# Two MLP stages: weights of the plain groups moved ahead of the operand sums, modulation steps spread, a last part of four tiles

## Chip, core and metric

One core of a Trainium2 chip (trn2) runs the whole program. The metric is the device time of one launch in microseconds, lower is better. Times of the kernel before are those of three runs, and one more execution was taken with the hardware profiler.

## The reference, cut to what matters

Two layers run over 640 positions: 128 context tokens and 512 latent tokens, which share the weights but have modulation vectors of their own. Everything is float32. The change touches only the second half of each layer, the gated MLP:

```python
xn2 = rmsnorm(x, norm2) * (1 + scale2) + shift2          # 640 x 1024
u   = dwconv3(xn2 @ w_up, ffn_conv_w)                    # w_up: 1024 x 5632, width-3 conv over positions
a, bval = u[..., :D_FF], u[..., D_FF:]                   # D_FF = 2816
x   = x + gate2 * ((silu(a) * bval) @ w_down)            # w_down: 2816 x 1024
```

and, inside layer 0's MLP, a part of the modulation vector of layer 1, `silu(c) @ w_ada[1] + b_ada[1]`, of which six blocks of 128 rows (blocks 10 to 15) are computed there. What stands ahead of the MLP (adaLN norm, recurrence, short convolution, attention, merge, output projection) is the same in both kernels.

## The kernel before, in words

**Layout.** Activations are kept transposed, channels on the 128 partitions and positions along the free axis; a matmul has 320 positions (half of them) as moving columns. To keep float32 accuracy every operand and every weight is split into a high part (a cast to fp32r on ScalarE) and a low part (a subtraction on VectorE); a product is three matmuls, high*high, high*low, low*high. The helper `split` (lines 115 and 116) does both halves, for weights into the tiles `whi` and `wlo` (six buffers each), for operands into `Xh`/`Xl` and `Fh`/`Fl`, for the activated MLP tiles into `fh`/`fl`. Weights land in four raw buffers `wraw` (two more, `T`, in the MLP), all issued from SyncE's queue in order.

**Queues.** The source is written as one sequence with generators that are advanced by hand (`next`, `run`). The framework plans at build time in which order each engine gets its instructions: an earlier place in the source is a higher priority, but an instruction whose inputs or buffer are not ready in the plan is passed by a later one. On the chip each engine then follows its planned order and waits for semaphores.

**The MLP stage** has 22 tiles of 128 hidden channels, each a pair of column groups of `w_up` (a and b).
- *Operand forms.* The two position halves of the normed input are B11, B21 (first half, computed at the end of the output projection) and B12, B22 (second half, `second`). Pairs from number 2 on use a seven-product scheme (`pair_steps`) that needs sums of the forms: T3, t2, T4, t1, each of two tiles and each split; they too are made in `second`. Six buffers `Fh`/`Fl` hold B12, T3, t2 and T4; T4 takes the buffers that B12 leaves.
- *Plain groups.* Pairs 0 and 1 (`PLAIN = 2`), four groups n = 0 to 3, are plain products over B11, B21, B12, B22 (lines 1211 to 1222): group n loads its weights at its first half and calls `finish` after its second. `finish(j, s)` is the width-3 convolution of one group (`ffn_conv`: one ScalarE, two VectorE instructions) and, with the second group of a pair, `ffn_act` (silu, product, split), which appends a tile to `Ys`.
- *Pairs.* `pair_steps` loads four raw tiles, adds them in place on VectorE (line 500) and splits seven weights a pair; it stops at three places, so that a pair's first product can be put ahead of the pair before it.
- *Down products.* `FFPARTS` cuts the 22 tiles into parts. When a part is complete its contributions to all eight output blocks (`down_steps`) run in the next part's pairs, are scaled on ScalarE (line 1232, tile `g`) and added to `x` in memory by a DMA from GpSimd. The last part is different: its eight blocks run at the end, for the first half of the positions in the order 0 to 7 and for the second half in the order 7, 6, 0 to 5, straight into `x` (line 1265), mixed with the norm of the next layer or the output. Its weights for blocks 0 to 4 are loaded and split twice, once for each half.
- *Modulation steps.* `ada_rows` makes 12 steps in layer 0's MLP, each a raw tile `in_w_rows` and two VectorE instructions that multiply and sum (line 318), and a short thirteenth. Two are taken after each pair (line 1248). Half way the vector tile `rows` is loaded again.

**PSUM.** The MLP has two banks for `Y`, one each for `Z` and `X`, two `f`, and the two `lin` that serve all stages.

Of the kernel before, what the change touches and what calls it, by code (L numbers as in the profile page):

```python
# [16 lines left out]
P = 128  # L17
# [29 lines left out]
AHEAD = (1, 4)  # L47
ADA1 = 10
ADAM = 3
FFPARTS = ((0, 3), (3, 7), (7, 11), (11, 15), (15, 19), (19, 22))  # L50

G_HG, G_CONV, G_CQ, G_CKV, G_KR, G_GATE, G_OUT, G_UP = 0, 20, 32, 35, 37, 38, 62, 70
NG = 70 + 2 * NFF
# [3 lines left out]
def hybrid_flow_kernel(ctx: ExitStack, tc: tile.TileContext, a: dict):  # L57
# [20 lines left out]
    def run(steps, n=None):  # L78
        while n is None or n > 0:
            try:  # L80
                next(steps)
            except StopIteration:
                return
            if n is not None:
                n -= 1
# [44 lines left out]
    def weights(srcs, keep=None):  # L130

        W = []
        for src in srcs:
            n = src.shape[-1] // P
            wh, wl = load_w(src, n * P, keep)
            W += [(wh[:, i * P:(i + 1) * P], wl[:, i * P:(i + 1) * P]) for i in range(n)]
        return W
# [269 lines left out]
    class Forms:  # L407
# [33 lines left out]
        def second(self, pool):  # L441
            bc = self.sq.rstd(1)
            raw = self.raw
            for q in range(2):
                for n, name in enumerate(("B12", "B22")):
                    f = raw[name, q] = form_tile(pool, F32, "fh", "xn", FHB)
                    for e in range(2):
                        norm_raw(self.l, self.which, self.sq, 1, f, e, KH * n + 2 * q + e, bc)
                    self.put(name, q, f)
            for q in range(2):  # L450
                f = raw["T3", q] = form_tile(pool, F32, "fl", "xs", FHB)
                V.tensor_tensor(f, raw["B22", q], raw["B12", q], ALU.subtract)
                self.put("T3", q, f)
            for q in range(2):
                f = raw["t2", q] = form_tile(pool, F32, "fl", "xs", FHB)
                V.scalar_tensor_tensor(f, raw["T3", q], -1.0, raw["B11", q], ALU.mult, ALU.subtract)
                self.put("t2", q, f)
            for q in range(2):
                f = raw["t2", q]
                V.scalar_tensor_tensor(f, f, -1.0, raw["B21", q], ALU.mult, ALU.subtract)  # L460
                self.put("T4", q, f)
            for q in range(2):
                f = raw["B12", q]
                V.tensor_tensor(f, raw["B11", q], f, ALU.subtract)
                self.put("t1", q, f)
            raw.clear()
# [69 lines left out]
    KEEP = KD - 3  # L536
# [453 lines left out]
    with pool_of("ap") as ap:  # L990
        rows, W, R = ada_load(ap)
# [68 lines left out]
    for l in range(DEPTH):  # L1060
# [4 lines left out]
        with pool_of("yp") as yp:  # L1065
            yB = [yp.tile([P, T + 1], F32, tag="yB", name="yB", bufs=4) for _ in range(4)]
            yC = [yp.tile([P, T], F32, tag="yC", name="yC", bufs=4) for _ in range(4)]
            with pool_of("cp") as cp, pool_of("kp") as kp:
# [10 lines left out]
                W = [mla_weights(l, 0)]  # L1079
# [15 lines left out]
            with pool_of("zp") as zp:  # L1095
# [11 lines left out]
                steps = iter(())  # L1107
# [15 lines left out]
                with pool_of("hp") as hp:  # L1123
                    if l == 0:
                        steps = chain(ada_rows(0, 16, 48, zp, lambda: ps.one("ad")),
                                      ada_rows(1, 0, ADA1, zp, lambda: ps.one("ad")))
                    else:
                        steps = ada_rows(1, 16, 48, zp, lambda: ps.one("ad"))
# [30 lines left out]
        xf = xf_.__enter__()  # L1159
        F = Forms(l, 1, sq, xf)  # L1160

        def kept(m):

            if not 0 < m <= KEEP:
                return None
            pool, tags, n = (xf, "F", 6) if m <= 3 else (wo, "k", 4)
            return lambda: [pool.tile([P, T], R32, tag=tags + t, name="keep", bufs=n) for t in "hl"]

        with pool_of("wo") as wo:
            W = {}  # L1170
# [16 lines left out]
        with pool_of("fp") as fp:  # L1187
            F.second(fp)
            sq = Squares(sq.pool)
            steps = iter(())  # L1190
            if l == 0:
                steps = ada_rows(1, ADA1, 16, fp, lambda: fp.tile([P, TP], F32, tag="u", name="pr", bufs=4)[:, 0:512])
            fconv = fp.tile([P, 3, 2 * NFF], F32, name="fconv")
            nc.sync.dma_start(fconv, a["fconv"][:, l])
            os_ = [fp.tile([P, TP + 2], F32, name=f"o{i}") for i in range(4)]
            zs = fp.tile([P, TP + 2], F32, name="z")
            for t in os_ + [zs]:
                for c0, c1 in ((0, 1), (TC + 1, TC + 3), (TP + 1, TP + 2)):
                    G.memset(t[:, c0:c1], 0.0)
            Ys, us = [], {}  # L1200

            def finish(j, s):
                us[s] = ffn_conv(s * NFF + j, os_[2 * (j % 2) + s], fp, fconv)
                if len(us) == 2:
                    Ys.append(ffn_act(us[0], us[1], fp))
                    us.clear()


            B = [F.operand("B11", "B21"), F.operand("B12", "B22")]
            held = {}  # L1210
            for n, j, tag in ((0, 0, "lin"), (1, 0, "lin"), (2, 0, "Y"), (0, 1, "Y"), (1, 1, "X"), (2, 1, "Z"),
                              (3, 0, "f"), (3, 1, "f")):
                if j == 0:
                    held[n] = weights(w_main(l, G_UP + n))
                o = (ps.bank() if tag == "lin" else ps.one(tag))[:, 0:HALF]
                for k, ((wh, wl), (xh, xl)) in enumerate(zip(held[n], B[j], strict=True)):
                    PE.matmul(o, wh, xh, start=(k == 0), stop=False)
                    PE.matmul(o, wh, xl, start=False, stop=False)
                    PE.matmul(o, wl, xh, start=False, stop=(k == KD - 1))
                put_half(os_[n], o, j)  # L1220
                if j == 1:
                    finish(n // 2, n % 2)

            def down_steps(k0, k1):
                for m in range(KD):
                    W = weights([a["w_down"][l, m][:, k * P:min(k + 4, k1) * P] for k in range(k0, k1, 4)])
                    g = fp.tile([P, T], F32, tag="u", name="g", bufs=4)
                    for j in range(2):
                        o = ps.any()
                        down_product(o[:, 0:FHALF[j].stop - FHALF[j].start], W, Ys[k0:k1], j)  # L1230
                        for c, s0, s1, s in FSEGS[j]:
                            S.mul(g[:, s0:s1], o[:, c:c + s1 - s0], modT[l][:, 40 + m, s:s + 1])  # L1232
                    G.dma_start(x[m], g, accum_op=ALU.add)  # L1233
                    yield

            ups = [pair_steps(l, G_UP + 2 * j, F, fp, os_[2 * (j % 2)], os_[2 * (j % 2) + 1], zs,
                              lambda s, j=j: finish(j, s)) for j in range(NFF)]
            next(ups[PLAIN])
            down = iter(())
            for pi, (k0, k1) in enumerate(FFPARTS):  # L1240
                last = pi == len(FFPARTS) - 1
                ahead = max(k0, PLAIN)
                for j in range(ahead, k1):
                    next(ups[j])
                    if j + 1 < NFF:
                        next(ups[j + 1])
                    run(ups[j])
                    run(steps, 2)
                    run(down, -(-KD // max(1, k1 - ahead - 1)))
                run(down)  # L1250
                if not last:
                    down = down_steps(k0, k1)
                if l == 0 and last:
                    run(steps)
                    ada_scale(1, 0)
            k0, k1 = FFPARTS[-1]
            W = {}
            for j in range(2):
                for m in both_ways(j):
                    if j == 0 or 0 <= m <= KEEP - 1:  # L1260
                        W[m] = weights([a["w_down"][l, m][:, k * P:min(k + 4, k1) * P] for k in range(k0, k1, 4)])
                    o = ps.any()
                    down_product(o[:, 0:FHALF[j].stop - FHALF[j].start], W[m], Ys[k0:k1], j)
                    for c, s0, s1, s in FSEGS[j]:
                        V.scalar_tensor_tensor(x[m][:, s0:s1], o[:, c:c + s1 - s0],
                                               modT[l][:, 40 + m, s:s + 1], x[m][:, s0:s1], ALU.mult, ALU.add)
                    sq.add(m, j)
                    if j == 1:
                        run(first, 1)
                if j == 0:  # L1270
                    if l + 1 < DEPTH:
                        X = new_X()
                        first = norm_steps(l + 1, 0, sq, 0, X)
                    else:
                        first = out_steps(sq, 0)
            run(first)
            if l + 1 < DEPTH:
                ps.phase("mla")
                run(norm_steps(l + 1, 0, sq, 1, X))
            else:  # L1280
                run(out_steps(sq, 1))
# [125 lines left out]
```

## Time and profile before

| what | value |
|---|---|
| median of three runs (lowest, highest) | 2590.28 us (2584.23, 2593.17) |
| the profiled execution, its own time | 2585.24 us |
| its span, first to last instruction | 2583.5 us |
| TensorE busy, share of the span | 2491.8 us, 96% |
| VectorE busy | 1853.4 us, 72% |
| ScalarE busy | 1333.6 us, 52% |
| MLP of layer 0, about | 846 to 1328 us of the span |
| MLP of layer 1 with the output, about | 2115 to 2583 us |

Times in the trace count from the span's start. A busy share says little on its own here: TensorE's matmuls overlap, and a stage's limit is read from the waits inside it. Line numbers (L116) are those of the listing above; PE is TensorE, DVE VectorE, ACT ScalarE, SP SyncE's queue.

### The profile page before, as it was taken

To read this page: it belongs to the slowest core of one execution; us is meant where nothing else is said; L and a number is where in the kernel's file an instruction comes from. 1 tells how busy PE (TensorE), PEld (TensorE's weight loads), DVE (VectorE), ACT (ScalarE), POOL (GpSimd) and SP (SyncE) were. 2 spreads that over 40 slices of the span, in tenths; PEclk is the share of its full clock that TensorE was granted. 3 is DMA by queue.
4 is the path that set the end of the run, shared out by engine and by line. 5 is a ranking of instruction groups with operands and counts; after the bars stand their busy time and mean duration, and the time that the engine had idled before them with its cause. 6 is when DMAs were issued, how large, how long until landed. Compare 5 with 4: busy or idle time off the path is not lost.

```text
span 2583.5 us, 44707 instructions
## 1 busy us (share of the span) xinstructions
PE 2491.8 (96%) x16942; PEld 2429.8 (94%) x16942; DVE 1853.4 (72%) x3711; ACT 1333.6 (52%) x2846; POOL 186.7 (7%) x207
## 2 busy tenths in 40 slices
PE   7999999999999899999989999999999999999997
PEld 3999999999999889999989999999999999999996
DVE  5677787787755778777677778777784468877775
ACT  3476733333324556666654766333433346766663
POOL 1000000000110000000120000000011110001011
PEclk8999999999999999999989999999999999999998
DMA  6211243333353154545432113433332323455443
GB/s 233 74 46 46 66 133 110 105 113 109 112 156 99 47 134 124 130 104 126 113 121 67 38 46 93 119 112 119 104 104 79 110 66 87 113 120 114 117 112 90
DMA packets 147498, 265.41 MB, mean 103 GB/s; under 512 B 17425, under 2 KB 32465, under 8 KB 147153
## 3 DMA queue, kind: packets, MB, share of 16 engines
q1 hardware_dynamic: 131154, 225.85, 29.5%
q0 software_dynamic: 11520, 26.22, 5.6%
q10 hardware_dynamic: 4608, 10.49, 1.3%
q8 instruction: 133, 2.18, 0.4%
q14 instruction: 83, 0.68, 0.1%
HBM read 229.68 MB, written 6.59 MB: 91 GB/s over the span
## 4 chain that ended last, share of the span: by engine, by line
PE 81%; DVE 11%; DMA 2%; ACT 2%; issue 2%; POOL 0%; DVEq 0%; SPq 0%; ACTq 0%; POOLq 0%
PE lin L148 13%; PE lin L150 13%; PE lin L149 13%; PE Y L472 3%; PE Y L474 3%; PE Y L473 3%; PE sc L625 2%; PE sc L890 2%; PE lin L978 2%; PE f L980 2%; PE lin L979 2%; PE lin L980 2%; PE f L979 2%; PE f L978 2%; DVE wlo L116 2%
## 5 line engine op out<-in xcount | busy, mean ns | idle before, releaser
L148 PE MATMUL lin<-Xh,whi 128*128 128x320 f32 x1920 | 605.1, 315 | 6.4 <-DVE th L728 5.1
L149 PE MATMUL lin<-Xl,whi 128*128 128x320 f32 x1920 | 595.4, 310 | 0.5 <-POOL Xl L379 0.5
L150 PE MATMUL lin<-Xh,wlo 128*128 128x320 f32 x1920 | 595.1, 310 | 0.0
L115 ACT CAST whi<-wraw 128x512 fp32r<-128x512 f32 (+1 forms) x578 | 349.0, 606 | 445.3 <-PE lin L149 270.7
L116 DVE TENSOR_TENSOR wlo<-wraw,whi 128x512 fp32r<-128x512 f32 (+1 forms) x578 | 389.0, 677 | 183.8 <-ACT whi L115 178.4
L148 PEld LDWEIGHTS lin<-Xh,whi 128*128 128x128 f32 x1920 | 361.3, 188 | 8.8 <-DVE th L728 6.9
L149 PEld LDWEIGHTS lin<-Xl,whi 128*128 128x128 f32 x1920 | 361.2, 188 | 0.8 <-POOL Xl L379 0.8
L150 PEld LDWEIGHTS lin<-Xh,wlo 128*128 128x128 f32 x1920 | 360.8, 188 | 0.0
L318 DVE SCALAR_TENSOR_TENSOR ad<-wraw,rows 128x512 f32<-128x512 f32 x296 | 211.6, 715 | 92.2 <-DMA wraw<-in_w_rows 88.7
L116 DVE TENSOR_TENSOR wlo<-T,whi 128x512 fp32r<-128x512 f32 x160 | 109.7, 688 | 71.5 <-ACT whi L115 70.6
L472 PE MATMUL Y<-Xh,whi 128*128 128x320 f32 x480 | 148.6, 310 | 2.5 <-ACT o L481 2.5
L474 PE MATMUL Y<-Xh,wlo 128*128 128x320 f32 x480 | 148.3, 309 | 0.0
L473 PE MATMUL Y<-Xl,whi 128*128 128x320 f32 x480 | 148.1, 309 | 0.0
L115 ACT CAST whi<-T 128x512 fp32r<-128x512 f32 x160 | 99.0, 621 | 82.5 <-DVE T L500 21.4
L1233 POOL DMA_DIRECT2D x<-g x80 | 69.2, 864 | 772.9 <-ACT g L1232 765.3
L148 PE MATMUL lin<-yh,whi 128*128 128x320 f32 x384 | 120.5, 314 | 0.7 <-ACT th L722 0.7
L978 PE MATMUL lin<-fh,whi 128*128 128x322 f32 (+1 forms) x352 | 111.0, 315 | 9.3 <-ACT fh L115 7.0
L150 PE MATMUL lin<-yh,wlo 128*128 128x320 f32 x384 | 118.8, 309 | 0.0
L149 PE MATMUL lin<-yl,whi 128*128 128x320 f32 x384 | 118.6, 309 | 0.0
L980 PE MATMUL lin<-fh,wlo 128*128 128x322 f32 (+1 forms) x352 | 110.9, 315 | 0.0
L979 PE MATMUL lin<-fl,whi 128*128 128x322 f32 (+1 forms) x352 | 110.8, 315 | 0.0
L980 PE MATMUL f<-fh,wlo 128*128 128x320 f32 (+1 forms) x352 | 110.3, 313 | 0.0
(377 smaller groups left out, 6335.6 us busy)
## 6 DMA issues: line engine op xcount, KB each, us to landing
wraw<-in_w_main SPq DMA_DIRECT2D x416, 256.0 KB, 2.7
wraw<-in_w_rows SPq DMA_DIRECT2D x160, 256.0 KB, 2.8
x<-g POOLq DMA_DIRECT2D x80, 320.0 KB, 4.7
wraw<-in_w_down SPq DMA_DIRECT2D x64, 256.0 KB, 2.8
wraw<-in_w_o SPq DMA_DIRECT2D x48, 256.0 KB, 2.7
T<-in_w_main SPq DMA_DIRECT2D x40, 256.0 KB, 2.9
wraw<-in_w_down SPq DMA_DIRECT2D x42, 192.0 KB, 2.4
ada<-in_w_ada SPq DMA_DIRECT2D x24, 256.0 KB, 6.0
```

Source lines behind the costliest of these rows:

```text
L115: S.copy(hi, x)
L116: V.tensor_tensor(lo, x, hi.bitcast(F32), ALU.subtract)
L148: PE.matmul(o, wh, xh[:, half(j)], start=(k == 0), stop=False)
L149: PE.matmul(o, wh, xl[:, half(j)], start=False, stop=False)
L150: PE.matmul(o, wl, xh[:, half(j)], start=False, stop=(k == n - 1))
L318: V.scalar_tensor_tensor(spare(), raw, 1.0, rows[:, s], ALU.mult, ALU.mult, accum_out=part[:, j, m - m0, s:s + 1])
L472: PE.matmul(o, wh[:, c], xh, start=start and k == 0, stop=False, skip_group_check=True)
L473: PE.matmul(o, wh[:, c], xl, start=False, stop=False, skip_group_check=True)
L474: PE.matmul(o, wl[:, c], xh, start=False, stop=stop and k == KH - 1, skip_group_check=True)
L978: PE.matmul(o, wh, fh[:, FHALF[j]], start=(k == 0), stop=False)
L979: PE.matmul(o, wh, fl[:, FHALF[j]], start=False, stop=False)
L980: PE.matmul(o, wl, fh[:, FHALF[j]], start=False, stop=(k == n - 1))
```

## The change

1. `Forms.second` ends after the four forms B12 and B22; the sums and their splits become a method `sums`, called after the loop over the plain groups. So the plain groups' loads and splits stand ahead of the sums in the source.
2. The plain loop no longer calls `finish`. Pair 0's two convolutions come after `sums`, pair 1's after pair 2's first product.
3. In layer 0 the modulation steps are taken one after each pair from pair 3 on, in place of two after each pair from pair 2 on.
4. The last two parts of `FFPARTS` are (15, 18) and (18, 22) in place of (15, 19) and (19, 22).
5. In the last part each block's weights are one load of four tiles, made once; blocks 1 to 5 are held in the six `Fh`/`Fl` buffers of the forms (`kept` with its new argument), and the second half loads nothing.

```diff
-FFPARTS = ((0, 3), (3, 7), (7, 11), (11, 15), (15, 19), (19, 22))
+FFPARTS = ((0, 3), (3, 7), (7, 11), (11, 15), (15, 18), (18, 22))
...
                     self.put(name, q, f)
+
+        def sums(self, pool):
+            raw = self.raw
             for q in range(2):
                 f = raw["T3", q] = form_tile(pool, F32, "fl", "xs", FHB)
...
-        def kept(m):
+        def kept(m, n0=3):
...
-            pool, tags, n = (xf, "F", 6) if m <= 3 else (wo, "k", 4)
+            pool, tags, n = (xf, "F", 6) if m <= n0 else (wo, "k", 4)
...
                 put_half(os_[n], o, j)
-                if j == 1:
-                    finish(n // 2, n % 2)
+            F.sums(fp)
...
+            for n in range(2):
+                finish(0, n)
             next(ups[PLAIN])
+            for n in range(2):
+                finish(1, n)
...
                     run(ups[j])
-                    run(steps, 2)
+                    if j >= FFPARTS[1][0]:
+                        run(steps, 1)
                     run(down, -(-KD // max(1, k1 - ahead - 1)))
...
-                    if j == 0 or 0 <= m <= KEEP - 1:
-                        W[m] = weights([a["w_down"][l, m][:, k * P:min(k + 4, k1) * P] for k in range(k0, k1, 4)])
+                    if j == 0:
+                        W[m] = weights([a["w_down"][l, m][:, k0 * P:k1 * P]], kept(m, KEEP))
```

## Rows read from the trace of the kernel before

**Rows 1.** The page, part 1: engine, busy us (share of span), instructions.
```profile
PE 2491.8 (96%) x16942; PEld 2429.8 (94%) x16942; DVE 1853.4 (72%) x3711; ACT 1333.6 (52%) x2846; POOL 186.7 (7%) x207
```

**Rows 2.** Busy time by stretch: stretch, length, engines busy (instructions), clock, DMA.
```profile
870.00:883.00 13.00, 8.24 (x40) 7.98 (x39) 11.33 (x17) 6.66 (x11) 0.00 (x0) 0.74 0.11 41
902.00:913.00 11.00, 7.28 (x30) 6.79 (x29) 9.13 (x18) 5.34 (x10) 0.00 (x0) 0.69 0.43 130
913.00:1003.00 90.00, 80.81 (x527) 78.48 (x526) 69.54 (x126) 53.31 (x122) 7.04 (x8) 0.98 0.50 131
1003.00:1289.00 286.00, 286.00 (x1943) 285.84 (x1942) 207.95 (x326) 184.45 (x409) 27.75 (x35) 1.00 0.51 119
1289.00:1299.00 10.00, 6.52 (x32) 5.99 (x31) 6.38 (x14) 4.92 (x11) 0.90 (x2) 0.83 0.08 21
2139.00:2150.00 11.00, 6.25 (x33) 5.99 (x33) 10.75 (x16) 5.97 (x9) 0.00 (x0) 0.84 0.14 48
2150.00:2537.00 387.00, 387.00 (x2630) 386.84 (x2629) 287.63 (x443) 256.58 (x568) 34.53 (x40) 1.00 0.48 116
2537.00:2548.00 11.00, 7.52 (x34) 7.26 (x33) 6.56 (x15) 4.86 (x10) 1.53 (x2) 0.69 0.06 18
```

**Rows 3.** Timeline, TensorE: start, us, instruction, [idle before <-releaser].
```profile
876.25 0.64 PE L1219 MATMUL f<-Xh,wlo 128*128 128x320 f32 x1 [4.76 <-DVE wlo L116]
...
886.72 0.31 PE L472 MATMUL Z<-Fh,whi 128*128 128x320 f32 x1
...
958.52 0.41 PE L472 MATMUL Y<-Xh,whi 128*128 128x320 f32 x1 [2.52 <-ACT o L481]
958.77 0.30 PE L473 MATMUL Y<-Xl,whi 128*128 128x320 f32 x1
958.91 0.31 PE L474 MATMUL Y<-Xh,wlo 128*128 128x320 f32 x1
...
2154.41 0.31 PE L472 MATMUL Z<-Fh,whi 128*128 128x320 f32 x1
```

**Rows 4.** Timeline, ScalarE and VectorE, layer 0, plain groups.
```profile
862.45 0.62 ACT L115 CAST whi<-wraw 128x512 fp32r<-128x512 f32 x1 [0.24 <-PE Y L1218]
...
866.04 0.61 ACT L115 CAST whi<-wraw 128x512 fp32r<-128x512 f32 x1
...
875.51 1.29 DVE L116 TENSOR_TENSOR wlo<-wraw,whi 128x512 fp32r<-128x512 f32 x2
```

**Rows 5.** The chain that ended last: start, us, what; first norm of either layer.
```profile
853.07 2.84 DVE xn L403 x6
...
2121.88 2.84 DVE xn L403 x6
```

**Rows 6.** VectorE by line and shape, 846 to 912 us: count, busy us, mean ns.
```profile
L116 DVE TENSOR_TENSOR wlo<-wraw,whi 128x512 fp32r<-128x512 f32 x8 | 5.4, 687 | 0.3 <-ACT whi L115 0.2
L959 DVE SCALAR_TENSOR_TENSOR u<-o,fconv,u 128x642 f32<-128x642 f32 x6 | 5.2, 884 | 0.9 <-ACT u L958 0.9
...
L116 DVE TENSOR_TENSOR Xl<-xn,Xh 128x640 fp32r<-128x640 f32 x4 | 3.3, 819 | 0.0
L318 DVE SCALAR_TENSOR_TENSOR pr<-wraw,rows 128x512 f32<-128x512 f32 x4 | 2.7, 685 | 0.0
```

**Rows 7.** Timeline, SyncE's queue, 936 to 990 us.
```profile
945.84 0.38 SPq L313 DMA_DIRECT2D rows<-c_keep  x1
...
970.01 5.02 SPq L316 DMA_DIRECT2D wraw<-in_w_rows  x2
```

**Rows 8.** Timeline, TensorE, first wait of layer 0's last part.
```profile
1293.60 0.41 PE L978 MATMUL lin<-fh,whi 128*128 128x322 f32 x1 [3.48 <-ACT fh L115]
```

**Rows 9.** Timeline, end of layer 1: VectorE and TensorE.
```profile
2556.31 0.56 DVE L116 TENSOR_TENSOR wlo<-wraw,whi 128x384 fp32r<-128x384 f32 x1
...
2561.29 0.94 PE L249 MATMUL lin<-dg,ones 128*128 128x128 f32 x6 [1.70 <-DVE dg L243]
```

## The prediction, made before the changed kernel ran

> **What bounds the kernel now.** I read the page first. TensorE is busy for 96% of the span, VectorE for 72% [rows 1]: the time is TensorE's list of matmuls plus the places where it stands still, and the change adds and removes no matmul. So the next view is the busy time by stretch [rows 2]. In the long undisturbed stretches (1003 to 1289 in layer 0, 2150 to 2537 in layer 1) TensorE never idles, the granted clock is 1.00, and 1943 matmuls in 286.0 us give 0.147 us a matmul. A stretch that holds n matmuls and is longer than 0.147 n has lost the rest, idle time and half-speed matmuls together. By this rule the MLPs lose
>
> - 870 to 883: 13.0 - 40 x 0.147 = 7.1 us, and 2139 to 2150 in layer 1: 6.1;
> - 902 to 913, layer 0 only: 6.6;
> - 913 to 1003, layer 0 only: 90.0 - 527 x 0.147 = 12.4;
> - 1289 to 1299: 5.3, and 2537 to 2548: 6.0.
>
> Together 43.5 us, all in places that the change touches. The timeline says what TensorE waited for [rows 3, 8]: the low half of group 3's weights, which VectorE had not made (4.76 us); in the last part the last activated tile (3.48 us). The half speed is seen in the clock of these stretches, 0.62 to 0.84 [rows 2]: after waits of 3.5 us and more matmuls run at the 1.2 GHz level for a while, while after the 2.52 us wait at 958 the second step is back at 0.14 us [rows 3].
>
> **A. Plain groups.** Group 3's first cast ended at 863.07 and its second at 866.65, but VectorE subtracted only at 875.51 [rows 4]: the sums, their splits and pair 0's convolution stood in between. With the weights ahead in the source this wait goes. But it does not follow that 7.1 and 6.1 us are won, since VectorE has worked without a break from its first norm at 853.07 (2121.88 in layer 1) [rows 5] and is next in line. What it must do before pair 2's first product over T3 can start: 8 norms at 2.84/6 = 0.47, 3.8 us; 4 splits of B12 and B22, 8 sums, 6 splits of T3, t2 and t1, all 640 wide, 18 at 0.82, 14.7; group 3's two weights at 0.69, 1.4; pair 0's convolutions and activation, 4 at 0.88 and 2 at 0.82, 5.2; half of pair 1's, 1.8; pair 2's first weights, split, add, split, 2.1 [rows 5, 6]. That is 29.0 us, so the product can start at 882.1 and 2150.9, against 886.72 and 2154.41 now [rows 3]: 4.6 + 3.5 = **8.1 us**. Ends: nothing (all of it comes back a product later), and 13.2 (pair 1's convolution stays behind and the plan hides the rest).
>
> The rule that speaks against this part is in the Trainium skill: "TensorE: Matmul & The Clock Gate", section "Architectural detail: the array is 16× 32×32, not 1× 128×128", says that ScalarE and VectorE take instructions in strict order. By that rule a subtraction put early in the queue holds up the sums behind it while its cast is missing, and the time would be that of rival 3 below. The trace agrees with the order itself: the subtraction ran 8.9 us after its last cast had ended.
>
> **B. The steps after pair 2.** From 902 to 913 TensorE lost 6.6 us at pair 3's third product, whose weights VectorE made late: four modulation instructions of 0.69 us, with their read-outs 3.1 us, stood in front [rows 2, 6]. Layer 1 has no such steps and loses nothing from 2150 on [rows 2]. The change takes none before the end of pair 3. Ends: 3.1, the instructions' own length, and 6.6. Layer 1 speaks for the upper end, TensorE's earlier arrival from A against it; I take **5.5 us**.
>
> **C. The steps after later pairs.** They are the same 24 instructions and the same 12 raw loads, moved from two after each of pairs 2 to 7 to one after each of pairs 3 to 14. VectorE in the undisturbed stretch works 208.0 of 286.0 us [rows 2] with 14 pairs, 20.4 us each; one step (1.5 us) lifts its share from 73 to 80%, two lift it to 88%. What hides a step is this free quarter of VectorE. A raw buffer is the other price: SyncE's queue stood 5.0 us over two such loads [rows 7], and behind them wait the pairs' weights. And the vector tile is loaded again half way, once, in either kernel; its load at 945.84 stands before the 2.52 us wait at 958 [rows 3, 7]. I leave 2.8 us for that (wait and first step) and 0.1 us for each of the 12 steps, 4.0 of the 12.4: **8.4 us** won. Ends: 0 and 12.4.
>
> **D. Last part.** Its weights come as one 512-wide load, split once, into buffers that the forms leave; if those come free in time, nothing waits for them. While the last tile is activated, TensorE can run what does not need it: four open sums (two `lin`, two `f`) of two tiles each now, of three then, 12 matmuls more; I count nine, as one sum may run ahead of the pair's last product. So the 3.48 us wait [rows 8] becomes 3.48 - 9 x 0.147 = 2.2, a length after which the clock stayed [rows 3]. The losses of 5.3 and 6.0 become 2.2 each: **6.9 us**. Ends: 0 and 11.3. The part before it has three tiles for four; the sum of down products, evictions and DMAs to `x` stays.
>
> **E. The reload that goes.** Five loads and splits in each second half fall away. At the end of layer 1 VectorE splits two of them (0.56 us) inside the chain of small instructions whose result TensorE then awaits for 1.70 us [rows 9]; layer 0's end is built alike. I take 1.0 a layer, **2.0 us**; ends 0 and 3.4.
>
> **Sum.** 8.1 + 5.5 + 8.4 + 6.9 + 2.0 = 30.9 us. The profiled execution took 2585.2 (span 2583.5); from it 2554.3. The median of the runs lies 5.0 above it, 2590.3, and I predict medians: 2559.
>
> **Rivals.**
> 1. *The wait only moves on.* VectorE is the bound from 853 to the end of pair 3; the plan then puts the missing time before pair 2's and pair 3's later products, or leaves group 3's subtraction behind the sums after all, since they are ready first (the change does not do what it says). A gives 0, B its lower end 3.1: 20.4 won, 2570. For it: VectorE busy 10.75 of 11 us from 2139 to 2150; against it: one pair later layer 1 runs without a wait [rows 2].
> 2. *Every wait goes.* The upper ends of A to E, 46.9 us: 2543. For it: 43.5 us are all the MLPs lose; against it: A's count of 29.0 us.
> 3. *The early subtraction blocks VectorE.* If it stands at the queue's head from the first cast's end, 863.07, to the second's, 866.65 [rows 4], less its own 0.69, VectorE loses 2.9 us a layer where it is the bound: 5.8 back, 2565. The Trainium skill's rule cited under A is this one.
> 4. *The kept weights come late.* If the forms' buffers are not free before the last pair ends, three of the four sums open now (18 matmuls, 2.6 us) are missing as cover in each layer: D turns from +6.9 to -5.2, 2571.
> 5. *Slower: a raw buffer is held in twelve pairs instead of six.* There are four for six to seven loads a pair, and the queue is in order. Two steps cost 6.6 us at pair 3; a step that cost half of it, 3.3, wherever it stands, makes 12 x 3.3 = 39.6 us in place of the 19.0 that B and C lose now, and with A, D and E (17.0) won the time is 2594. The kernel is slower from 3.0 us a step on. Against it: between 913 and 1003 the eight steps after pairs 3 to 6 cost 12.4 us with the reload, 1.2 us each without its 2.8.
>
> **How the numbers follow.** Chances: my sum 0.45, within 2550 to 2567; rival 1 0.20; rival 2 0.10; rival 3 0.09; rival 4 0.08; rival 5 0.08, of which half ends above the old time and half close to it. A difference of 0.3% (7.8 us) is about what a measurement of this kernel can tell from none. Slower 0.05, with a little for mishaps of the plan elsewhere; the same 0.07, from rival 5's better half and the low ends of B to D together; faster 0.88. The range runs from rival 2, 2542, past rivals 1 and 4, to 2577.
>
> **What would show each step right or wrong.** A: the 4.8 us waits at the plain groups' fourth group are gone in both layers, and waits of about 2 us, if any, stand before pair 2's products; a wait as long as before there is rival 1, an idle VectorE before the subtraction is rival 3. B and C: no wait over 3 us in pairs 3 to 8 and a clock of 1.00 there; small waits in each pair up to 14, and SyncE's queue held by `in_w_rows`, are rival 5. D: the wait at the last part about 2 us with full clock behind it; casts into the kept buffers that come after the last pair's products are rival 4. E: no weight splits in the second half. The sum is wrong most easily in C, where the plan's order decides, and in A, where I trust a count.

## The result, and the profile after

The changed kernel takes 2553.61 us (median of four runs, 2551.23 to 2555.63) against 2587.26 (four runs, 2582.93 to 2593.17) for the one before: a ratio of 0.9868, 95% interval 0.9844 to 0.9892. By the medians that is 33.7 us, by the two profiled executions 31.3 (spans of 2583.5 and 2552.2 us). The forecast was 31 us and 2559, with a range from 2542 to 2577. The sum is right; its parts are not, as the stretches show.

Part 1 of the page after (engine, busy us and share of the span, instructions):

```profile
PE 2478.7 (97%) x16942; PEld 2418.3 (95%) x16942; DVE 1846.7 (72%) x3701; ACT 1326.0 (52%) x2836; POOL 185.0 (7%) x207
```

The matmuls are as many as before, so a stretch is again read by its length less 0.147 us a matmul, which is what it lost. Busy time by stretch of the kernel after (columns as in [rows 2]), from plain groups to pair 2, pair 3, pairs 3 to 8, the long stretch, the last part, the end of layer 0's MLP, all that lies between the MLPs, and then the same for layer 1:

```profile
871.00:899.00 28.00, 25.69 (x172) 24.94 (x171) 27.15 (x41) 20.44 (x40) 0.00 (x0) 1.00 0.12 39
899.00:903.00 4.00, 4.00 (x30) 4.00 (x29) 4.00 (x8) 2.33 (x6) 0.00 (x0) 1.00 0.19 51
903.00:985.00 82.00, 78.65 (x527) 77.26 (x526) 67.50 (x116) 55.04 (x127) 7.03 (x8) 1.00 0.53 136
985.00:1260.00 275.00, 274.82 (x1859) 273.82 (x1858) 209.15 (x343) 178.50 (x401) 27.50 (x32) 1.00 0.52 130
1260.00:1281.00 21.00, 17.60 (x114) 16.59 (x113) 14.64 (x29) 10.29 (x21) 3.46 (x4) 1.00 0.30 92
1281.00:1318.60 37.60, 34.80 (x234) 33.06 (x233) 27.92 (x80) 21.00 (x52) 11.32 (x15) 1.00 0.33 111
1318.60:2098.20 779.60, 769.26 (x5387) 755.23 (x5387) 534.09 (x1166) 355.55 (x744) 40.75 (x41) 1.00 0.30 89
2119.00:2151.00 32.00, 29.70 (x189) 28.96 (x188) 29.62 (x47) 21.24 (x46) 0.00 (x0) 0.95 0.20 60
2151.00:2224.00 73.00, 71.03 (x479) 70.24 (x478) 57.67 (x91) 49.01 (x113) 6.89 (x8) 1.00 0.51 127
2224.00:2499.00 275.00, 275.00 (x1867) 275.00 (x1866) 202.45 (x311) 182.03 (x402) 27.54 (x32) 1.00 0.50 118
2499.00:2522.00 23.00, 21.27 (x139) 20.28 (x138) 14.73 (x29) 10.56 (x21) 3.46 (x4) 1.00 0.12 39
2522.00:2552.20 30.20, 19.04 (x128) 18.12 (x126) 18.14 (x54) 4.12 (x9) 3.42 (x4) 0.81 0.26 88
```

Three stretches of the kernel before that [rows 2] do not hold: the end of layer 0's MLP, what lies between the MLPs, the end of the program:

```profile
1299.00:1345.00 46.00, 39.85 (x234) 37.72 (x233) 34.49 (x95) 22.87 (x56) 14.29 (x14) 0.89 0.44 144
1345.00:2122.50 777.50, 768.06 (x5388) 753.76 (x5387) 535.19 (x1167) 357.88 (x750) 42.52 (x42) 1.00 0.30 89
2548.00:2583.50 35.50, 20.37 (x132) 18.95 (x131) 23.67 (x68) 6.55 (x15) 5.58 (x7) 0.83 0.27 91
```

Length less 0.147 us a matmul, before and after, in us:

| stretch | term | before | after | won | forecast |
|---|---|---|---|---|---|
| plain groups to pair 2, layer 0 and layer 1 | A | 7.1 + 6.1 | 2.7 + 4.2 | 6.3 | 8.1 |
| pair 3, layer 0 | B | 6.6 | 0 | 6.6 | 5.5 |
| pairs 3 to 8 and the long stretch, layer 0 | C | 12.4 + 0.4 | 4.5 + 1.7 | 6.6 | 8.4 |
| last part, layers 0 and 1 | D | 5.3 + 6.0 | 4.2 + 2.6 | 4.5 | 6.9 |
| behind the last part, layers 0 and 1 | E | 11.6 + 16.1 | 3.2 + 11.4 | 13.1 | 2.0 |
| pairs of layer 1 | none | 0.4 | 2.6 + 0.6 | -2.8 | 0 |
| between the MLPs | none | | | -2.2 | 0 |
| ahead of the first MLP (first norm at 853.07 and 854.08) | none | | | -1.0 | 0 |

These add up to 31.1 us. (The 0.4 us of the long stretches before are what the rounding of the rate to 0.147 leaves there.) A to C won 19.5 where 22.0 stood, D and E 17.6 where 8.9 stood, and 6.0 us were lost in places that no term has. Between the MLPs, but for the first 10 us, every engine has the same instructions in the same order in both traces, so those 2.2 us are not a new plan (see the last section).

The main waits that are left where the change works, in TensorE's timeline of the kernel after (the second column is the duration, in brackets the idle time before and what ended it): pair 2's product over T3 in each layer, the last activated tile in each layer, and, without a wait now, the matmul on the next norm's diagonal at the end of layer 0.

```profile
882.73 0.41 PE L475 MATMUL Z<-Fh,whi 128*128 128x320 f32 x1 [2.31 <-ACT whi L115]
2126.22 0.41 PE L475 MATMUL Z<-Fh,whi 128*128 128x320 f32 x1 [2.31 <-ACT whi L115]
1271.54 0.42 PE L981 MATMUL lin<-fh,whi 128*128 128x322 f32 x1 [2.40 <-ACT fh L115]
2511.62 0.41 PE L981 MATMUL lin<-fh,whi 128*128 128x322 f32 x1 [1.19 <-ACT fh L115]
1289.46 0.38 PE L249 MATMUL lin<-dg,ones 128*128 128x128 f32 x1
```

The 4.76 us waits of [rows 3] are gone, the 3.48 us of [rows 8] are 2.40 and 1.19, and the diagonal, for which TensorE waited 1.70 us, finds no idle time before it. The wait for the second half's diagonal at the very end of the program stays as it was, 3.02 us in both traces.

### The profile page after: what moved, and what is told of

Same layout as the page of the kernel before. It is cut to its first block, busy times and chain, and to the rows that moved or that the text cites. A ratio compares the mean times of both kernels' runs of the same rounds, so it can differ in the third digit from the quotient of the medians.

```text
span 2552.2 us, 44650 instructions
## 1 busy us (share of the span) xinstructions
PE 2478.7 (97%) x16942; PEld 2418.3 (95%) x16942; DVE 1846.7 (72%) x3701; ACT 1326.0 (52%) x2836; POOL 185.0 (7%) x207
## 4 chain that ended last, share of the span: by engine, by line
PE 81%; DVE 10%; DMA 4%; ACT 3%; issue 2%; POOL 0%; DVEq 0%; SPq 0%; ACTq 0%; POOLq 0%
PE lin L148 13%; PE lin L149 13%; PE lin L150 13%; PE Y L475 3%; PE Y L477 3%; PE Y L476 3%; PE sc L628 2%; PE sc L893 2%; PE lin L981 2%; PE lin L982 2%; PE f L982 2%; PE f L981 2%; PE f L983 2%; PE lin L983 2%; DVE wlo L116 2%
## 5 line engine op out<-in xcount | busy, mean ns | idle before, releaser
L115 ACT CAST whi<-wraw 128x512 fp32r<-128x512 f32 (+2 forms) x558 | 337.8, 607 | 414.7 <-PE lin L149 268.9
L116 DVE TENSOR_TENSOR wlo<-wraw,whi 128x512 fp32r<-128x512 f32 (+2 forms) x558 | 375.1, 678 | 163.1 <-ACT whi L115 157.1
L981 PE MATMUL lin<-fh,whi 128*128 128x322 f32 (+1 forms) x320 | 100.3, 314 | 5.0 <-ACT fh L115 3.6
L475 PE MATMUL Z<-Fh,whi 128*128 128x320 f32 x320 | 99.4, 311 | 4.7 <-ACT whi L115 4.6
L982 PE MATMUL lin<-fl,whi 128*128 128x322 f32 (+1 forms) x320 | 99.7, 311 | 0.0
L983 PE MATMUL lin<-fh,wlo 128*128 128x322 f32 (+1 forms) x320 | 99.5, 311 | 0.0
```

What stands on the lines that cost most here:

```text
L115: S.copy(hi, x)
L116: V.tensor_tensor(lo, x, hi.bitcast(F32), ALU.subtract)
L475: PE.matmul(o, wh[:, c], xh, start=start and k == 0, stop=False, skip_group_check=True)
L981: PE.matmul(o, wh, fh[:, FHALF[j]], start=(k == 0), stop=False)
L982: PE.matmul(o, wh, fl[:, FHALF[j]], start=False, stop=False)
L983: PE.matmul(o, wl, fh[:, FHALF[j]], start=False, stop=(k == n - 1))
```

## The experiments

Each kernel ran beside the kernel before on the same chip; ratios are to that one. `no_t1` ran once, all others four to eleven times.

**Each part alone on the kernel before.**

```diff
# a_plain: sums() after the plain loop, finish(0, n) behind it,
#          finish(1, n) after pair 2's first product
# c_steps
-                    run(steps, 2)
+                    if j >= FFPARTS[1][0]:
+                        run(steps, 1)
# d_four
-FFPARTS = ((0, 3), (3, 7), (7, 11), (11, 15), (15, 19), (19, 22))
+FFPARTS = ((0, 3), (3, 7), (7, 11), (11, 15), (15, 18), (18, 22))
# e_kept
-                    if j == 0 or 0 <= m <= KEEP - 1:
-                        W[m] = weights([a["w_down"][l, m][:, k * P:min(k + 4, k1) * P] for k in range(k0, k1, 4)])
+                    if j == 0:
+                        W[m] = weights([a["w_down"][l, m][:, k0 * P:k1 * P]], kept(m, KEEP))
```

> The kernel before with part A alone (plain groups' weights ahead of the operand sums, convolutions after them). In the changed kernel the plain groups' loss fell by 4.5 us in layer 0 and 2.3 us in layer 1. Theory 1, the parts add up: 6.8 us, a ratio of 0.9974, and the loss of 6.8 us at pair 3's third product stays as it was. Rival, VectorE passes the time on while the modulation steps still stand behind pair 2: the 4.5 us of layer 0 come back at pair 3, whose loss grows from 6.8 to about 11, and only layer 1's 2.3 us are won, 0.9991.

Measured: 1.0005 (0.9996 to 1.0014). Nothing is won; the rival is nearer. TensorE's waits from 850 to 1000 say why in layer 0 (engine, tile, line, releaser: us in total, times, longest):

```profile
PE Y L475 <- ACT whi L115: 10.2, 2, 5.6
PE Z L475 <- ACT whi L115: 2.5, 2, 2.3
```

The wait for group 3's low half is gone; 2.3 us at pair 2 have come, and `Y`'s waits for a cast, two of them, are longer, up to 5.6 us. From behind the wait at pair 2 (880) to 912, layer 0 loses 32.0 - 152 x 0.147 = 9.7 us, where it lost 6.6 at pair 3 before, as the rival has it. What the MLPs did win was lost between them, where this run took 781.9 us for the same 5388 matmuls (777.5 before).

> The kernel before with parts B and C alone (one modulation step after each pair from pair 3 on). The changed kernel lost 6.7 us less at pair 3 and 8.1 us less in pairs 3 to 8 than the kernel before. Theory 1, the steps cause these losses by themselves: 14.8 us, a ratio of 0.9943. Rival, a good part came with part A, which lets VectorE reach pair 2 earlier: with A missing the lower end of B, 3.1 us, and about half of C, 4, are won, 7 us, 0.9973, with waits over 2 us left in pairs 3 to 7.

Measured: 0.9962 (0.9949 to 0.9974), 9.8 us, between the two; the time does not decide. The stretches do. Pair 3, pairs 3 to 8, and all between the MLPs:

```profile
882.80:905.90 23.10, 23.10 (x159) 23.10 (x159) 21.90 (x36) 17.08 (x38) 0.00 (x0) 1.00 0.30 93
905.90:986.90 81.00, 78.55 (x527) 77.29 (x526) 65.79 (x112) 53.74 (x123) 7.03 (x8) 1.00 0.48 127
1328.70:2110.70 782.00, 770.19 (x5387) 755.19 (x5387) 534.88 (x1167) 357.73 (x750) 42.29 (x42) 1.00 0.28 89
```

Pair 3 loses nothing (6.6 before) and pairs 3 to 8 lose 81.0 - 527 x 0.147 = 3.5 us (12.4 before): 15.5 us won without part A, as theory 1 says, and no wait over 2 us left there. 4.5 us of it are missing again between the MLPs, where the edit is not.

> The kernel before with four tiles in the last part and three in the one before it, the second half's weights still loaded again. In the changed kernel the last part and what follows it lost about 8.5 us less in layer 0 and 8 us less in layer 1. Theory 1 (as predicted), four tiles cover only the last tile's activation and the reload is a term of its own: 5 us, 0.998, and the wait for the diagonal of the next norms (1.70 us) stays. Rival, longer down products also cover the chain of the next norms after the first half: 12 us or more, 0.9953, and the wait for the diagonal is gone.

Measured: 0.9952 (0.9939 to 0.9964), 12.4 us. The rival has it. At the end of layer 0's MLP the longest waits are these; none is left for the first norm's diagonal (`lin`, L249), only 1.9 us for the second one's (`pt`):

```profile
PE lin L978 <- ACT fh L115: 2.2, 1, 2.2
PE pt L249 <- DVE dg L243: 1.9, 1, 1.9
...
```

> The kernel before with the second half's weights kept, three tiles in the last part as before. Theory 1 (as predicted), the reload's splits stand in the chain of small VectorE instructions and cost 1 us a layer: 2 us, 0.9992. Rival one, the reload is what made the end of layer 0 slow by way of ScalarE's and VectorE's queues: 10 us, 0.996, and the half-speed matmuls after the wait for the diagonal are gone. Rival two, the gain at the end comes from the four tiles: 0 to 1 us, 1.000. The wait of 3.48 us for the last activated tile stays in all of them.

Measured: 0.9971 (0.996 to 0.9983), 7.5 us, nearest to rival one. In the same stretch the wait for the diagonal is 1.1 us, and the one for the last activated tile is not 3.48 but longer:

```profile
PE lin L978 <- ACT fh L115: 4.6, 1, 4.6
PE lin L249 <- DVE dg L243: 1.1, 1, 1.1
```

The four ratios add up to 1.1% (28 us) against 1.3% for the change. That is no proof of independent parts: D and E, as the traces show, work on the same end.

**Parts taken out of the change.**

```diff
# no_a: the changed kernel with the old second(), finish(n // 2, n % 2) in the plain loop
# no_e: the changed kernel with the second half's weights loaded again
```

> The changed kernel without part A (sums and convolutions stand ahead of the plain groups' last weights again; B to E stay). Part A alone changed nothing (1.0005), although the waits at the plain groups were gone in its trace. Theory 1, A pays only where the modulation steps no longer stand behind pair 2: without it the changed kernel loses the 4.5 us of layer 0 and part of the 2.3 us of layer 1, about 6 us, 0.989 to 0.9895 against the kernel before. Rival, what A wins at the plain groups is lost again at the next pairs in either case (layer 1, which has no steps, lost 2.8 us more there): no more than 3 us, 0.9868 to 0.988.

Measured: 0.9882 (0.9864 to 0.99); the changed kernel has 0.9868 with intervals that overlap. By the ratios A is worth 3.6 us here, nearer to the rival than to the 6 us of theory 1, but the intervals leave room for both. The traces speak for the rival. From the plain groups to pair 8, without A:

```profile
867.00:983.00 116.00, 108.87 (x724) 107.43 (x723) 99.06 (x163) 77.88 (x170) 7.05 (x8) 0.99 0.41 112
2110.00:2224.00 114.00, 109.23 (x734) 108.98 (x733) 97.61 (x152) 79.46 (x173) 6.91 (x8) 0.99 0.40 105
```

That is 9.6 us lost in layer 0 and 6.1 in layer 1; with A it is 114.0 us for 724 matmuls (871 to 985), 7.6 lost, and 105.0 us for 666 (2119 to 2224), 7.1 lost. So A wins 2.0 us in layer 0 and loses 1.0 in layer 1 (by the second execution of the changed kernel, below, 1.0 and 0.3). The waits give the two sides: those of TensorE in layer 1, from 2090 to 2230 or 2240, without A and then with it (left out is the first norm's diagonal, 1.2 us in both):

```profile
PE f L1219 <- DVE wlo L116: 4.8, 1, 4.8
...
```

```profile
PE Z L475 <- ACT whi L115: 2.3, 1, 2.3
...
PE Y L475 <- ACT o L484: 0.9, 1, 0.9
PE lin L981 <- ACT g L1234: 0.9, 1, 0.9
```

4.8 us in one wait became 4.1 in three. In layer 0, too, the pairs take some back: without A pairs 3 to 8 lose 3.2 us (a stretch of 81.00 us with 529 matmuls), with it 4.5.

> The changed kernel with the second half's weights loaded again (A to D stay). Alone the four tiles were worth 0.9952 and the kept weights 0.9971. Theory 1, both shorten the same chain at the end of the MLPs (the next norms' diagonal and what waits for it), so that the kept weights are worth less beside the four tiles: by the traces of the single parts 4 to 5 us, 0.9885 against the kernel before. Rival, the two add up: 7.5 us, 0.9897.

Measured: 0.9885 (0.9869 to 0.9901). By the ratio E is worth 4.4 us beside the four tiles, as theory 1 has it, but the intervals overlap here too; the waits at the end of layer 0 agree, as they are those of `d_four` again (2.1, 1.9, 1.4 and 0.9 us).

**Why A is worth so little: VectorE's list, or what comes after?**

```diff
# t1_pool
-                V.tensor_tensor(f, raw["B11", q], f, ALU.subtract)
-                self.put("t1", q, f)
+                G.tensor_tensor(f, raw["B11", q], f, ALU.subtract)
+                self.put("t1", q, f, G)        # split's low part on GpSimd too
# no_t1
-            (the four lines that make t1)
+            self.f["t1"] = self.f["B11"]
```

> The changed kernel with the differences t1 and their low parts on GpSimd instead of VectorE: four of its 0.8 us instructions a layer less before pair 2's product over T3 (3.2 us). Theory 1, VectorE's list is the bound from the first norm to pair 2: the waits of 2.31 and 2.30 us there go, and those in the next pairs shrink too: 4.5 to 8 us faster than the changed kernel, 0.984 to 0.985 against the kernel before. Rival, the plan's order or ScalarE's casts set the wait: 0 to 2 us, 0.986 to 0.987, the wait stays over 1.5 us.

Measured: 0.9885 (0.9869 to 0.99), no gain. The 2.31 us wait did go, but a row of waits up to 0.9 us took its place. VectorE's convolutions from 850 to 900, with the changed kernel first (line 962 has another six, 896 and 1318 ns; mean ns is the last number before the second bar):

```profile
L963 DVE SCALAR_TENSOR_TENSOR u<-o,fconv,u 128x642 f32<-128x642 f32 x6 | 5.4, 896 | 0.0
```

```profile
L963 DVE SCALAR_TENSOR_TENSOR u<-o,fconv,u 128x642 f32<-128x642 f32 x6 | 7.8, 1319 | 0.0
```

GpSimd took 3.2 us off VectorE's list and 12 x 0.42 = 5.1 us were put on it. The move did not test the theory; leaving the work out does so better:

> The changed kernel without the two t1 operands: their differences and their splits are left out (four VectorE instructions of 0.8 us and two ScalarE casts a layer), and the pairs' products over t1 take the operand B11 instead, so the products are as many but the values are others. Moving this work to GpSimd did not help: VectorE's 642-wide convolutions took 2.15 us beside GpSimd in place of 0.90. Theory 1, VectorE's list is the bound from the first norm to pair 2: with 3.2 us less and no GpSimd work beside it the waits of 2.3 us there shrink below 0.5 in both layers. Rival, ScalarE's casts or the order set the wait: it stays over 1.5 us.

Measured: 2542.98 us, one run, beside a median of 2583.88. Theory 1 holds in the trace: from the plain groups through pair 2 TensorE is busy without a break in both layers. Two casts of ScalarE went with the work, so the two engines are not fully told apart; but from 853 to 883 of the changed kernel VectorE is busy for 28.97 of 30 us and ScalarE for 24.54.

```profile
867.50:893.00 25.50, 25.50 (x176) 25.39 (x174) 24.44 (x37) 18.78 (x38) 0.00 (x0) 1.00 0.15 42
2109.00:2130.00 21.00, 21.00 (x144) 20.89 (x144) 19.93 (x31) 16.18 (x33) 0.00 (x0) 1.00 0.15 48
```

> The changed kernel once more, to see which of its waits come back in a second execution. Theory 1, the waits of 0.92 and 0.94 us in layer 1's pairs and those of pairs 3 to 8 are late landings of single loads, which change from one execution to the next though every engine's order is the same: some are gone and others are there. Rival, they belong to part A's order: they stand at the same places with the same lengths within 0.1 us. The time: 0.987 against the kernel before.

Measured: 0.9868 (0.9855 to 0.9882). Each theory has a part. In layer 0's pairs 3 to 8 all five waits over 0.3 us come back at the same products, four of them within 0.05 us (1.40 for 1.38) and one shorter (0.24 for 0.64); in layer 1 that of 0.92 us is gone, that of 0.94 came back as 0.93, and one of 0.57 is new. So the places belong to the plan, and only some lengths to the landing of single loads.

**What holds the pairs: raw buffers, for the most part.** Two of these versions are also meant to be faster.

```diff
# halves: conv, activation and split of the last pair in two ranges of columns
+                cuts = ((0, HALF + 1), (HALF + 1, TP)) if j == NFF - 1 else ((0, TP),)
# halves_rd1: halves, and the fourth weight tile of a pair in a buffer of its own
+                 pool.tile([P, 512], F32, tag="rd", name="rd", bufs=1) if rd else
-            rd = load(wd)
+            rd = load(wd, rd=True)
# two_late: the kernel before, no step after pair 2
+                    if j >= FFPARTS[1][0]:
                         run(steps, 2)
```

> The changed kernel with the last pair's convolutions, activation and split made in two halves of columns, so that after the last eviction only instructions of half the length follow. In the changed kernel 7.4 us pass from the last product's end to the last tile, and TensorE waits 2.40 us for it in layer 0 and 1.19 us in layer 1. Theory 1, the length of these instructions sets the wait: the chain shortens by about 3 us, both waits go, 3 to 3.6 us, 0.9855 against the kernel before. Rival, the shorter instructions cost as much in number, or the list stands behind others: under 1 us, 0.9868.

Measured: 0.9858 (0.9842 to 0.9873); not apart from 0.9868 by the intervals. The waits fell from 2.40 to 1.65 and from 1.19 to 0.33 us, 1.6 us in all, half of what theory 1 said: half the columns take 546 ns, not half of 896.

> The changed kernel with the last pair in two halves of columns, and with a raw buffer of its own for each pair's fourth weight tile (five raw buffers in the MLPs in place of four). In the changed kernel pairs 3 to 8 of layer 0 still lose 4.8 us and layer 1 2.8 us, where ScalarE or VectorE stand on a weight load that landed late. Theory 1, four raw buffers let the loads start too late: with a fifth these waits go, 5 to 7 us below the version with halves alone (0.9858), 0.983 to 0.984. Rival, the loads take their time in the DMA queues and not for want of a buffer: 0 to 2 us, 0.985 to 0.986.

Measured: 0.9836 (0.9822 to 0.9849), 2543.45 us, the fastest version here that leaves nothing out. By the ratios that is 5.7 us below `halves`, as theory 1 has it, though the intervals overlap a little. How a late load becomes a wait of TensorE is seen in SyncE's queue and ScalarE in the changed kernel (start, duration; the last row's casts read tiles issued by the second):

```profile
912.80 0.33 SPq L316 DMA_DIRECT2D wraw<-in_w_rows  x1
918.06 1.50 SPq L121 DMA_DIRECT2D wraw<-in_w_down  x3
```

```profile
923.30 0.92 ACT L115 CAST whi<-wraw 128x384 fp32r<-128x384 f32 x2 [3.81 <-PE Z L477]
```

After the step's raw tile the queue issues nothing for 5 us; the first down weights then land too late, at 923.20, ScalarE stands 3.81 us on their cast, the eviction of `Y` stands behind the cast, and TensorE waits 1.38 us for "ACT o". (The cast's row names TensorE's Z, which ended just then; but in the five other traces that have this wait, too, the cast starts 0.10 us after the landing, while TensorE's last update lies up to 0.8 us back.) With a fifth buffer pairs 3 to 8 of the same layer lose 1.3 us in place of 4.5, and layer 1's two waits of 0.9 are gone (of which one was gone in the second execution of the changed kernel, too):

```profile
901.80:980.60 78.80, 77.78 (x527) 77.24 (x526) 68.47 (x117) 55.90 (x127) 7.03 (x8) 1.00 0.56 142
```

But not all goes. In these pairs it is the four waits of 0.40 to 0.64 us that are gone. The largest is left, at the same product, where ScalarE still stands 3.15 us on the cast of down weights (TensorE's waits from 850 to 1000):

```profile
PE Y L475 <- ACT o L484: 1.0, 1, 1.0
```

Here the rival has a part: the load that ends this wait took about 5 us from issue to landing in both kernels, where down weights of this size take 2.6 at the median. Up to 917.11 GpSimd had issued three of its adds to `x`, 320 KB each, and from 916 to 925 their queue, q0, took most of the DMA engines' time (packets, MB, share; changed kernel):

```profile
q0 software_dynamic: 395, 0.89, 65.4%
q1 hardware_dynamic: 576, 0.85, 26.5%
```

That the adds hold this load up is read from the trace; adds at other times were not tried.

> The kernel before with part B alone: two modulation steps after each of pairs 3 to 8, none after pair 2. Together with C (one step after each of pairs 3 to 14) it was worth 0.9962. Theory 1 (as the prediction's terms have it), two steps after a pair cost in themselves, so only B's 6.7 us are won and pairs 4 to 9 lose about as much as pairs 3 to 7 did, 12 us: 0.998 to 0.9985. Rival, the losses came of the backlog that pair 2's steps left, and pairs 3 to 8 with two steps each lose under 5 us: 0.9955 to 0.9965.

Measured: 1.0004 (0.9995 to 1.0013), nothing, less than either theory gave. Pair 3 is clean (first row), and the pairs behind it lose it again (second row): two steps after a pair cost at these pairs, too. Below the stretches stand waits of ScalarE and TensorE behind 907:

```profile
884.40:907.60 23.20, 23.20 (x161) 23.20 (x160) 21.95 (x36) 17.06 (x37) 0.00 (x0) 1.00 0.31 93
907.60:1038.50 130.90, 117.99 (x759) 115.67 (x759) 99.83 (x181) 74.86 (x171) 11.33 (x13) 0.96 0.47 125
```

```profile
ACT whi L115 <- DMA wraw<-in_w_down: 13.7, 7, 4.4
...
PE Y L472 <- ACT whi L115: 5.0, 1, 5.0
```

130.9 - 759 x 0.147 = 19.3 us are lost, and up to 1020 ScalarE waited 13.7 us in seven waits for down weights that had not landed.

## Why the prediction was right, and where its steps were not

**The total** was 30.9 us forecast and 31.3 measured between the spans, and the time lies well inside the range; but two errors of opposite sign met in it: too much was credited to A to C, too little to D and E. That the sum came out so close is luck. (The lowest clock in [rows 2] is 0.69, not the 0.62 that the prediction reads there; nothing hangs on it.)

**A: the start was right, its worth was not.** The product over T3 was to start 29.0 us after the first norm; it starts 28.65 us after it in layer 0 (882.73 less the start of the row below) and 28.63 in layer 1; before it was 33.65 and 32.53:

```profile
854.08 0.55 DVE L403 SCALAR_TENSOR_TENSOR xn<-x,amul,lin 128x320 f32<-128x320 f32 x1 [1.03 <-PE lin L249]
```

That is 8.9 us earlier in all, where 8.1 stood. That the list of work sets this start is shown by `no_t1`, but for the two casts. The count's total is right in part by luck. Ahead of the product VectorE has 20 instructions of 640 columns and not 18 (T4's two splits are among them), and three of pair 1's convolutions and not two; but the count priced each at its whole duration, 0.82 us, while they start 0.735 us apart, each before the one ahead has ended:

```profile
862.16 1.56 DVE L116 TENSOR_TENSOR Fl<-xs,Fh 128x640 fp32r<-128x640 f32 x2
863.63 0.83 DVE L459 SCALAR_TENSOR_TENSOR xs<-xs,xn 128x640 f32<-128x640 f32 x1
```

20 x 0.735 is 14.7 us, as 18 x 0.82 is. By stretches only 6.3 us were won, as the clock takes some back behind the wait that is left. In layer 1 it fell to 0.88, and 13.78 - 81 x 0.147 = 1.9 us were lost there:

```profile
2126.22:2140.00 13.78, 13.78 (x81) 13.38 (x82) 11.62 (x21) 7.69 (x18) 0.00 (x0) 0.88 0.24 73
```

What failed is the step that credits the whole sum, as if nothing after pair 2 took it back: layer 1's pairs lose 2.8 us that they did not lose before, and the single part (with 4.4 us against it between the MLPs) and the part taken out both show a worth near nothing. This is rival 1 (chance 0.20), that the wait only moves on, by another mechanism: not VectorE's list but, for the most part, the raw buffers, since with a fifth one most of these waits are gone. That TensorE now comes to these pairs earlier than their loads is read from the traces. Whether A is worth its 6 us once there are five was not tried. Rival 3 did not come: VectorE is busy for 28.97 of the 30 us from 853 to 883, so the early subtraction holds up next to nothing, and the order rule of the Trainium skill cited under A does no harm here.

**B and C were nearly right in sum, but not for the reason given.** 13.2 us were won against 13.9. I costed the moved steps at 0.1 us each by VectorE's free quarter. `two_late` shows that spacing is what counts: with the same 24 instructions two to a pair the gain is nil, and what is late then are loads (13.7 us of ScalarE's waits). Two steps a pair leave VectorE idle for a quarter of that stretch (99.83 us busy of 130.9), so its free time is not what ran out; that the steps' raw tiles held the loads up is read from the trace and was not tried by itself. So rival 5's resource, the raw buffer, is real, but one step a pair costs at most 0.5 us and not 3.3: 6.2 us are left in twelve pairs, and a fifth buffer takes 3.2 of them. The 2.8 us that C left for the reload of the vector tile were not lost: the reload is issued at 1011.75, and TensorE waits nowhere over 0.25 us from there to 1262.

**D and E were sized at half.** The step that failed is in D, "the sum of down products, evictions and DMAs to `x` stays", and in E, "I take 1.0 a layer". I read the last part only as far as its first wait, 2537 to 2548, and took the 1.70 us wait of [rows 9] for all that follows. By the prediction's own rule the stretches behind it lost 11.6 + 16.1 = 27.7 us, which stand in no term and are missing from the 43.5 us of rival 2. But 4 tiles in place of 3 put 16 x 3 = 48 matmuls, 7.1 us, from the pairs to behind the last activation, and the second half's share of them runs while VectorE makes the first half's norm. `d_four` alone, with no weight kept, takes the wait for the diagonal away and wins 12.4 us, more than D and E together in the forecast. Kept weights alone win 7.5, also by that end; beside the four tiles 4.4 by the ratio, not well told from nothing. The nine matmuls of cover that D did count were near the truth: a wait of 2.2 us forecast, 2.40 and 1.19 measured, with the clock at 1.00 around them. That it is the second half's products that cover the norm's chain is read from the traces; it was not tried by itself.

**Rivals 2 and 4** did not come: 2.3 us waits stay, and the kept casts were in time. In `e_kept` the wait for the last tile grew by 1.1 us in layer 0 and fell to 2.8 in layer 1; whether the kept casts had a part in either was not tried.

## What to carry to other kernels

A stage's gain is worth what the next stage's buffers let through: after taking a wait out, look at the loads that are issued between the old and the new time of arrival. When work is moved to the end of a stage, follow the chain to the next stage's first matmul, not to the first wait; matmuls behind the last serial chain are cover, and cover can be made by cutting parts differently.

## What the runs showed of the hardware that was not expected

**The same wait, two clocks.** The prediction took 2.2 us as a length after which the clock stays. In two executions of the changed kernel, with the same order on TensorE, the wait at pair 2 is 2.31 and 2.30 us; behind the first the granted clock was 1.00, behind the second 0.88, and 68 matmuls ran in the 14 us that held 77 (stretches of 14 us that begin about 5.5 us ahead of the product; first execution, then second):

```profile
877.00:891.00 14.00, 11.69 (x77) 10.94 (x76) 13.22 (x21) 9.30 (x20) 0.00 (x0) 1.00 0.06 21
```

```profile
876.00:890.00 14.00, 11.70 (x68) 11.21 (x67) 11.90 (x20) 7.88 (x17) 0.00 (x0) 0.88 0.01 2
```

The 2.31 us wait in layer 1 of the first execution was followed by 0.88 as well (its row stands under A). In the second execution's layer 0, the first eight matmuls behind the wait ran at the 2.4 GHz level (the first three of them 0.25 us apart, as in the first execution, the others 0.15), the next thirteen 0.27 us apart (the 1.2 GHz level), and then 0.15 again: 1.4 us, with nothing in the order that tells the two apart.

**A stretch that no edit touches scatters by 5 us.** Between the MLPs, from the same matmul to the same matmul and with the same order on the engines, the traces took 777.5 us (before), 779.6 (after), 781.9 (`a_plain`), 782.0 (`c_steps`) and 776.8 (`no_e`). What sets it was not tried; differences of 2 to 4 us between single kernels here are read by stretches, not from the whole time.

**GpSimd and VectorE slow each other.** In `t1_pool` GpSimd's two differences took 6.4 us each (the same operation on the same size takes 1.6 to 1.9 elsewhere in that run), and VectorE's convolutions beside it 2.15 us in place of 0.90, while its sums of 640 columns beside GpSimd stayed at 0.81.

```profile
L733 POOL TENSOR_TENSOR h<-h,th 128x640 f32<-128x640 f32 x28 | 53.0, 1892 | 399.7 <-DVE th L731 399.7
...
L467 POOL TENSOR_TENSOR xn<-xn 128x640 f32<-128x640 f32 x4 | 25.4, 6370 | 32.0 <-DVE xs L455 32.0
```

The Trainium skill, "GPSIMD Engine Reference", section "1. Specifications", says that the two share SBUF interfaces and contend where a VectorE instruction has two inputs there; the trace agrees that they contend. Both the convolutions and the sums read two tiles of SBUF; why the ones were slowed and the others not is not settled here.
